# The last block's up-projection by seven Strassen products instead of eight, with the weight sums made in the blocks before

## The chip, the cores and the metric

The kernel runs on one core of a Trainium2 chip. The metric is the device time in microseconds of one execution, the median of several runs. Its engines are named as in the profile: PE is TensorE's matmul, PEld its weight load, DVE is VectorE, ACT is ScalarE, POOL is GpSimd, and SP is SyncE, from whose queue every DMA is issued.

## What is computed

The reference is one encoder layer over 2048 positions of 1024 channels: a norm, a windowed attention and a state-space mixer side by side, an output projection, and then a feed-forward part. The change is in the up-projection of the last part:

```python
h = rmsnorm(x, norm2_g[l])
u = dwconv(h @ w_up[l].astype(h.dtype), ffn_conv_w[l], ffn_conv_b[l])
gate, val = jnp.split(u, 2, axis=-1)
x = x + (jax.nn.silu(gate) * val) @ w_down[l].astype(h.dtype)
```

`h` has 1024 channels, `w_up` 2 x 2816 columns, and `dwconv` is a convolution over three positions. All is float32.

## The kernel before

Matmuls keep float32 accuracy by a split: each operand is a rounded part `hi` and a rest `lo`, and `mm3` (lines 106 to 108 of the profile) issues three matmuls, hi by hi, hi by lo and lo by hi, for each 128 channels.

The positions are cut into four blocks `j` of 512. For each block the feed-forward part goes through 22 pairs of 128 columns (one gate, one value). `up_mm` multiplies a pair's two weight tiles with the block's `h2` (8 chunks of 128 channels, so 2 x 8 x 3 = 48 matmuls over 512 positions) into two PSUM banks, tiles `up`. `up_unit` then makes the convolution from the banks: ACT writes the middle tap (line 1049), DVE adds the two others (line 1047, "taps", each out = u x weight + out) and the seam to the block before (from `hal`, one or two elements), ACT makes the tanh, DVE two products (lines 1070 and 1071) and, after a cast on ACT, the rest (line 1075). The result `f` goes into the down-projection `down_unit`, which adds to `x`. Pairs come in groups, and the down-projection of a group stands behind the up-projection of the next one. In the last block each down-projection is cut into halves of 258 and 256 positions (`down_part`, line 1111).

Weights come by DMA as 128x1024 tiles `wraw`. `w_split` makes `whi` on ACT (line 141) and `wlo` on POOL (line 142), two tiles ahead, in two buffers each. `wplan` lists the tiles in order, and `next_w` steps through it.

In blocks 0 to 2 the attention and state-space chunks of the following block are stepped in between by `pace`. At the end of a block `wo_unit` makes the output projection of the next one, and `h2_stage` its norm and the split of its `h2` (line 1022 and line 208), between the last down-projections. The last block has nothing after it but `final` of block 2 (line 1183), and it ends with `last_down`.

The order of the instructions on each engine is set when the program is built, by the framework's scheduler, from the order of the code and its own estimates. An engine executes its instructions strictly in that order.

Of the kernel before, what the change touches and what calls it, by code (L numbers as in the profile page):

```python
# [17 lines left out]
P = 128  # L18
# [39 lines left out]
def block_kernel(ctx: ExitStack, tc: tile.TileContext, a: dict, out: bass.AP):  # L58
# [31 lines left out]
    def dram(name, shape):  # L90
        return dpool.tile(shape, F32, tag=name, name=name)
# [922 lines left out]
    def h2_stage(j, ss):  # L1014
# [10 lines left out]
            split(hi[:, k], lo[:, k], t, eng(14) if k % 2 == 0 else eng(15))  # L1025
        h2[j] = (hi, lo)

    def up_mm(j, pr, ws):
# [48 lines left out]
        pend.append(tail)  # L1077

    def down_unit(j, g, cp, fs, w):
        k0, nk = GROUPS[g]  # L1080
        whi, wlo = w
        x1 = xone[j]
        if j < NB - 1:
            ps = new_mm(f"dn{j}_{g}_{cp}")
            for i in range(2):
                for k in range(nk):
                    kk = ksl(i * nk + k)
                    mm3(ps[i], whi[:, kk], wlo[:, kk], fs[:, k, 0, :TB], fs[:, k, 1, :TB], k == 0, k == nk - 1)
# [7 lines left out]
    PART = ((0, 258), (258, FW))  # L1096

    def down_part(j, g, c, b, fs, w):
        k0, nk = GROUPS[g]
# [94 lines left out]
    def w_wo():  # L1194
        return [(a["w_out"][c], 1024) for c in range(NK)]

    def w_dn(g):
        k0, nk = GROUPS[g]
        return [(a["w_dn"][cp][:, :, k0 * P : (k0 + nk) * P], 2 * nk * P) for cp in range(4)]

    def wo_pair(cp, s):
# [12 lines left out]
                wplan.append((a["w_ch"][int(tok[1:])], 1024))  # L1214
    wplan += [wo_pair(cp, 1) for cp in range(4)]
    wplan += [(a["w_ch"][c], 1024) for c in (11, 12)]
    for j in range(NB):
        for g, (k0, nk) in enumerate(GROUPS):
            wplan += [(a["w_up"][k0 + i, q], 1024) for i in range(nk) for q in range(2)]
            if g > 0:  # L1220
                wplan += w_dn(g - 1)
        if j + 1 < NB:
            wplan[-2:-2] = w_wo()
        wplan += w_dn(len(GROUPS) - 1)

    def step(streams, n=1):
        for _ in range(n):
# [138 lines left out]
    for j in range(NB):  # L1366
# [1 line left out]
        if j > 0:  # L1368
            mx = start_side(j + 1)
        fss = []  # L1370
        for g, (k0, nk) in enumerate(GROUPS):
# [127 lines left out]
```

## Time and profile before

| | us |
|---|---|
| median of 3 runs (2495.41 to 2500.74) | 2496.29 |
| the profiled execution, its own time | 2505.61 |
| its span, first to last instruction | 2503.8 |
| PE busy in the span | 2373.5 |
| DVE, ACT, POOL busy | 1761.6, 1088.3, 1126.9 |
| blocks 0 to 2 of the feed-forward part | 659 to 2110 |
| block 3 | 2110 to the end |

Busy time of PE is modelled and overlaps, so the rate of matmuls is read from start to start. Durations of POOL are rough. The spans of the blocks are read from the sequence of PE's tiles.

### The profile page before, as it was taken

What the parts mean: (1) busy time and instruction counts of PE and PEld (TensorE: products, weight loads), DVE (VectorE), ACT (ScalarE), POOL (GpSimd) and SP (SyncE); (2) the same over time, 40 slices, a digit from 0 to 9 for tenths busy, and PEclk for the clock granted to TensorE, in tenths of its full rate; (3) what the DMA queues carried; (4) which work ended last, traced back from release to release, by engine and by line L of the source; (5) the groups of instructions that cost most, each with busy time, mean ns of one, the idle gap of its engine ahead of it and who ended that gap; (6) DMA issues with size and microseconds to landing.
All of it is one profiled execution on the core that took longest, in us unless ns stands there. A gap on an engine that the chain in (4) does not pass through costs nothing.

```text
span 2503.8 us, 31565 instructions
## 1 busy us (share of the span) xinstructions
PE 2373.5 (95%) x11440; PEld 1975.7 (79%) x11440; DVE 1761.6 (70%) x3116; ACT 1088.3 (43%) x1814; POOL 1126.9 (45%) x625
## 2 busy tenths in 40 slices
PE   8998999887899999999999999999999999999997
PEld 6877798766688887777788777777888877788887
DVE  5778778878786775468978685689686555844445
ACT  5444565444354444335444443254444433433334
POOL 1045314564545435445444443554444445544444
PEclk9999999998899999999999999999999999999998
DMA  6567445774433343333434333343443232332232
GB/s 225 178 198 224 126 147 186 247 246 149 141 116 122 127 140 97 101 112 122 126 131 137 99 133 114 90 129 119 129 127 96 84 114 89 118 101 93 93 94 84
DMA packets 176047, 332.13 MB, mean 133 GB/s; under 512 B 13202, under 2 KB 84242, under 8 KB 175892
## 3 DMA queue, kind: packets, MB, share of 16 engines
q1 hardware_dynamic: 175892, 330.12, 41.2%
q8 instruction: 90, 1.47, 0.2%
q14 instruction: 65, 0.53, 0.1%
HBM read 284.06 MB, written 44.71 MB: 131 GB/s over the span
## 4 chain that ended last, share of the span: by engine, by line
PE 50%; DVE 9%; POOL 2%; issue 2%; ACT 1%; DMA 1%; DVEq 0%; POOLq 0%; SPq 0%; ACTq 0%
PE up_b L108 9%; PE up_b L107 9%; PE up_b L106 9%; PE dn_b L106 3%; PE dn_b L107 3%; PE dn_b L108 3%; DVE fa L1047 2%; POOL wlo L142 2%; PE dn L107 2%; PE dn L106 2%; PE dn L108 2%; PE wo_b L108 2%; PE wo_b L106 2%; PE wo_b L107 2%; DVE m_lo L972 1%
## 5 line engine op out<-in xcount | busy, mean ns | idle before, releaser
L142 POOL TENSOR_TENSOR wlo<-wraw,whi 128x1024 fp32r<-128x1024 f32 (+1 forms) x306 | 739.0, 2416 | 901.8 <-ACT whi L141 849.8
L108 PE MATMUL up_b<-h_hi,wlo 128*128 128x512 f32 x1392 | 555.3, 399 | 15.9 <-POOL wlo L142 15.8
L107 PE MATMUL up_b<-h_lo,whi 128*128 128x512 f32 x1392 | 553.0, 398 | 4.7 <-DVE h_lo L208 4.7
L106 PE MATMUL up_b<-h_hi,whi 128*128 128x512 f32 x1392 | 554.3, 399 | 1.4 <-ACT whi L141 0.9
L141 ACT CAST whi<-wraw 128x1024 fp32r<-128x1024 f32 (+1 forms) x330 | 338.9, 1027 | 453.0 <-PE up_b L107 117.8
L1047 DVE SCALAR_TENSOR_TENSOR fa<-up_b,fcw,fa 128x511 f32<-128x511 f32 (+2 forms) x396 | 271.4, 686 | 206.1 <-ACT fa L1049 201.7
L108 PEld LDWEIGHTS up_b<-h_hi,wlo 128*128 128x128 f32 x1392 | 264.6, 190 | 79.8 <-POOL wlo L142 21.8
L107 PEld LDWEIGHTS up_b<-h_lo,whi 128*128 128x128 f32 x1392 | 264.3, 190 | 63.3 <-DVE h_lo L208 5.9
L106 PEld LDWEIGHTS up_b<-h_hi,whi 128*128 128x128 f32 x1392 | 264.1, 190 | 60.1 <-ACT whi L141 2.3
L106 PE MATMUL dn_b<-f,whi 128*128 128x512 f32 x528 | 211.4, 400 | 0.4 <-DVE x L1090 0.2
L107 PE MATMUL dn_b<-f,whi 128*128 128x512 f32 x528 | 208.8, 395 | 0.0
L108 PE MATMUL dn_b<-f,wlo 128*128 128x512 f32 x528 | 204.3, 397 | 0.0
L1069 ACT ACTIVATE fth<-fa 128x512 f32<-128x512 f32 (+1 forms) x88 | 55.6, 632 | 217.3 <-DVE fa L1047 165.3
L1074 ACT CAST f<-fth 128x512 fp32r<-128x512 f32 (+1 forms) x88 | 54.4, 620 | 207.6 <-DVE fth L1071 169.2
L1090 DVE TENSOR_TENSOR x<-x,dn_b 128x512 f32<-128x512 f32 x144 | 97.5, 680 | 61.0 <-PE dn_b L108 60.9
L1049 ACT ACTIVATE fa<-up_b,fcw 128x512 f32<-128x512 f32 x176 | 136.0, 774 | 0.2
L106 PEld LDWEIGHTS dn_b<-f,whi 128*128 128x128 f32 x528 | 99.7, 189 | 22.8 <-DVE x L1090 1.1
L108 PEld LDWEIGHTS dn_b<-f,wlo 128*128 128x128 f32 x528 | 99.3, 188 | 22.4 <-POOL wlo L142 0.3
L107 PEld LDWEIGHTS dn_b<-f,whi 128*128 128x128 f32 x528 | 99.2, 188 | 21.2
L875 DVE SCALAR_TENSOR_TENSOR ab<-ab,ldt,mask 128x128 f32<-128x128 f32 x256 | 106.7, 482 | 11.7 <-DMA ab<-acs_d 11.5
L1075 DVE TENSOR_TENSOR f<-fth,f 128x512 fp32r<-128x512 f32 (+1 forms) x88 | 79.2, 900 | 30.3 <-ACT f L1074 29.4
L106 PE MATMUL pj_b<-h_hi,whi 128*128 128x512 f32 x208 | 85.4, 411 | 12.3 <-ACT h_hi L235 7.1
(328 smaller groups left out, 5047.1 us busy)
## 6 DMA issues: line engine op xcount, KB each, us to landing
wraw<-in_w_up SPq DMA_DIRECT2D x176, 512.0 KB
wraw<-in_w_dn SPq DMA_DIRECT2D x64, 512.0 KB
wraw<-in_w_out SPq DMA_DIRECT2D x36, 512.0 KB
ab<-acs_d SPq DMA_DIRECT2D x32, 512.0 KB
wraw<-in_w_ch SPq DMA_DIRECT2D x28, 512.0 KB
wraw<-in_w_dn SPq DMA_DIRECT2D x32, 384.0 KB
ak<-ks_d SPq DMA_DIRECT2D x14, 768.0 KB
cs<-in_rope SPq DMA_DIRECT2D x20, 512.0 KB
```

The costliest lines, as they stand in the source:

```text
L106: nc.tensor.matmul(ps, whi, xhi, start=first, stop=False)
L107: nc.tensor.matmul(ps, whi, xlo, start=False, stop=False)
L108: nc.tensor.matmul(ps, wlo, xhi, start=False, stop=last)
L141: A.copy(hi[:, :m], raw[:, :m])
L142: (V if i < WV or i in WVS else G).tensor_tensor(lo[:, :m], raw[:, :m], hi[:, :m].bitcast(F32), ALU.subtract)
L875: (G if i < SUBP[0 if first else 1] else V).scalar_tensor_tensor(ab[:, i, d], ab[:, i, d], ldt[:, d, c, h : h + 1], mask3[:, 2 * d * P : ( ...
L1047: V.scalar_tensor_tensor(o, src, w(q), o, ALU.mult, ALU.add)
L1049: A.activation(ai[:, 0:TB], u, AF.Identity, bias=w(3), scale=w(2))
L1069: A.activation(th[:, :n], acc[:, 0, :n], AF.Tanh)
L1074: A.copy(fs[:, idx, 0, :n], th[:, :n])
L1075: V.tensor_tensor(fs[:, idx, 1, :n], th[:, :n], fs[:, idx, 0, :n].bitcast(F32), ALU.subtract)
L1090: V.tensor_tensor(xv, xv, ps[i], ALU.add)
```

## The change

In block 3 two pairs make a "super" `s` (11 of them). Its weights are seen as a 2 x 2 matrix: gate or value by the first or second 512 channels. Its `h2` is a 2 x 2 matrix too: first or second 512 channels by first or second 256 positions. A Strassen scheme in Winograd's form makes the four result quarters from seven products. `up_super` issues them: each has 2 x 4 x 3 = 24 matmuls over 256 positions into one bank, with one 128x1024 weight tile. Three of the seven tiles are weights as they are, four are sums `S1` to `S4`. One copy on ACT and eight additions on DVE (line 1111 of the changed kernel; six take one bank each, one bank is taken twice) build the gate tile `us..g` and the value tile `us..v` in SBUF. `up_unit` is as before, but its input `u` is now such a tile, and the two units of a super are emitted inside the next super.

The weight sums are made on POOL in blocks 0 to 2, behind the split of a pair's value tile, for the pairs with `pr % 3 == j`: four operations of 128x512 for each of 22 pairs, and two DMAs to the scratch `ws_d`. `wraw` has three buffers instead of two. In block 3 weights are split three tiles ahead instead of two, and the third pair of buffers lies in the attention's. `h2_stage_w` makes the seven split combinations of `h2` for block 3 in place of the plain split. The groups of block 3 are of 4, 4, 4, 4, 4 and 2 pairs instead of 4, 4, 4, 4, 3 and 3. The DMA scratch of the program is set smaller.

```diff
+GROUPSW = [(0, 4), (4, 4), (8, 4), (12, 4), (16, 4), (20, 2)]
+PROD = (0, 2, 3, 1, 6, 4, 5)
...
-        raw = wpool.tile([P, 1024], F32, tag="wraw", name="wraw")
+        raw = wpool.tile([P, 1024], F32, tag="wraw", name="wraw", bufs=3)
...
+        elif i >= wdeep[0] and (i - wdeep[0]) % 3 == 2:
+            hi = bp.tile([P, H * P], F32R, tag="qs", name="whi3")
+            lo = bp.tile([P, 12 * P], F32R, tag="ks", name="wlo3")
...
+        if i in wsum:
+            gate, val = wraws[i - 1], raw
+            g0, g1, v0, v1 = gate[:, :512], gate[:, 512:], val[:, :512], val[:, 512:]
+            sa, sb = (sumpool.tile([P, 2, 512], F32, tag="wsum", name=f"ws{wsum[i]}{z}") for z in "ab")
+            G.tensor_tensor(sa[:, 0], v0, v1, ALU.add)
+            G.tensor_tensor(sa[:, 1], sa[:, 0], g0, ALU.subtract)
+            G.tensor_tensor(sb[:, 0], g0, v0, ALU.subtract)
+            G.tensor_tensor(sb[:, 1], g1, sa[:, 1], ALU.subtract)
+            nc.sync.dma_start(ws_d[wsum[i], :, 0:2], sa)
+            nc.sync.dma_start(ws_d[wsum[i], :, 2:4], sb)
...
+        if i >= wdeep[0]:
+            w_split(i + 2)
+            w_raw(i + 3)
...
+    def h2_stage_w(j, ss):
...
+            tt = t1024(f"h2s{j}_{k}").rearrange("p (z n) -> p z n", z=4)
+            V.tensor_tensor(tt[:, 0], b12, b11, ALU.subtract)
+            V.tensor_tensor(tt[:, 1], b22, tt[:, 0], ALU.subtract)
+            G.tensor_tensor(tt[:, 2], b22, b12, ALU.subtract)
+            G.tensor_tensor(tt[:, 3], b21, tt[:, 1], ALU.subtract)
+            split(pw[0][:, 0, 0, k], pw[0][:, 0, 1, k], b11, V)
+            split(pw[1][:, :, 0, k], pw[1][:, :, 1, k], tt[:, 0:2], V)
+            split(p6[0][k // 2][:, k % 2], p6[1][k // 2][:, k % 2], b21, V)
+            split(pw[2][:, :, 0, k], pw[2][:, :, 1, k], tt[:, 2:4], G)
+            split(pw[0][:, 1, 0, k], pw[0][:, 1, 1, k], b22, V)
...
+    def up_super(j, s, prev):
...
+            for pr in range(2):
+                for k in range(4):
+                    hi, lo = h2[j][PROD[q]][k]
+                    mm3(bank[:, pr], w[0][:, ksl(4 * pr + k)], w[1][:, ksl(4 * pr + k)], hi, lo, k == 0, k == 3)
...
+        A.copy(gl, product(0))
+        add(gr, gl, product(1))
+        if prev:
+            prev.pop(0)()
+        add(vl, gr, product(2))
+        ps = product(3)
+        add(vr, vl, ps)
+        add(gr, gr, ps)
+        add(gl, gl, product(4))
+        if prev:
+            prev.pop(0)()
+        add(gr, gr, product(5))
+        add(vl, vl, product(6))
```

What the built program makes of it is shown at three places. The first is DVE in block 3, in the convolution of a pair (`up3_9_b0` and `_b1` are its two banks, `fa` the convolution, `hal` the seam). Before:

```order
L1047 SCALAR_TENSOR_TENSOR fa3_9_18378<-up3_9_b0_18328,fcw_139,fa3_9_18378 128x510
L1047 SCALAR_TENSOR_TENSOR fa3_9_18378<-up3_9_b0_18328,fcw_139,fa3_9_18378 128x511
L1056 TENSOR_SCALAR fa3_9_18378<-up3_9_b0_18328,fcw_139 128x1
L1047 SCALAR_TENSOR_TENSOR fa3_9_18378<-hal_93,fcw_139,fa3_9_18378 128x2
L1047 SCALAR_TENSOR_TENSOR fa3_9_18378<-up3_9_b0_18328,fcw_139,fa3_9_18378 128x1
L1047 SCALAR_TENSOR_TENSOR fa3_9_18378<-hal_93,fcw_139,fa3_9_18378 128x1
L1070 SCALAR_TENSOR_TENSOR fth3_9_18396<-fth3_9_18396,fa3_9_18378 128x514
L1047 SCALAR_TENSOR_TENSOR fa3_9_18378<-up3_9_b1_18329,fcw_139,fa3_9_18378 128x510
L1047 SCALAR_TENSOR_TENSOR fa3_9_18378<-up3_9_b1_18329,fcw_139,fa3_9_18378 128x511
```

After the change, from the last addition of super 4 to the first of super 5 (`us3_4g` and `us3_4v` are its gate and value tiles, `us3_5_1` is the bank of the next super's product 1, `fa3_8` and `fa3_9` its two pairs' convolutions):

```order
L1111 TENSOR_TENSOR us3_4v_18836<-us3_4v_18836,us3_4_6_19080 128x2x256
L1147 SCALAR_TENSOR_TENSOR fa3_9_19291<-us3_4g_18835,fcw_143,fa3_9_19291 128x511
L1147 SCALAR_TENSOR_TENSOR fa3_8_19172<-hal_96,fcw_143,fa3_8_19172 128x2
L1147 SCALAR_TENSOR_TENSOR fa3_9_19291<-hal_96,fcw_143,fa3_9_19291 128x2
L1147 SCALAR_TENSOR_TENSOR fa3_8_19172<-hal_96,fcw_143,fa3_8_19172 128x1
L1147 SCALAR_TENSOR_TENSOR fa3_8_19172<-us3_4v_18836,fcw_143,fa3_8_19172 128x510
L1147 SCALAR_TENSOR_TENSOR fa3_9_19291<-hal_96,fcw_143,fa3_9_19291 128x1
L1147 SCALAR_TENSOR_TENSOR fa3_9_19291<-us3_4v_18836,fcw_143,fa3_9_19291 128x510
L1147 SCALAR_TENSOR_TENSOR fa3_8_19172<-us3_4v_18836,fcw_143,fa3_8_19172 128x511
L1147 SCALAR_TENSOR_TENSOR fa3_9_19291<-us3_4v_18836,fcw_143,fa3_9_19291 128x511
L1147 SCALAR_TENSOR_TENSOR fa3_8_19172<-hal_96,fcw_143,fa3_8_19172 128x2
L1111 TENSOR_TENSOR us3_5g_19106<-us3_5g_19106,us3_5_1_19146 128x2x256
```

The taps of a pair now read a tile in SBUF where they read a bank, and the rest of the taps of two pairs stands ahead of the addition that empties the bank of the next super's product 1.

The second place is POOL in block 0 (`wlo` is the split of a weight tile, `ws9a` and `ws9b` are the sums of pair 9, `y` and `arc` belong to the state-space mixer and the attention). Before:

```order
L142 TENSOR_TENSOR wlo_6675<-wraw_6626,whi_6674 128x1024
L900 TENSOR_TENSOR y6_7000<-xsbf6_6846,vecs_143 128x512
L142 TENSOR_TENSOR wlo_6723<-wraw_6678,whi_6722 128x1024
L142 TENSOR_TENSOR wlo_6762<-wraw_6726,whi_6761 128x1024
L796 TENSOR_TENSOR arc5_6840<-arc5_6840,mhalf_83 128x1
L142 TENSOR_TENSOR wlo_6768<-wraw_6765,whi_6767 128x1024
L142 TENSOR_TENSOR wlo_6879<-wraw_6771,whi_6878 128x1024
```

After the change:

```order
L158 TENSOR_TENSOR wlo_6703<-wraw_6654,whi_6702 128x1024
L929 TENSOR_TENSOR y6_7036<-xsbf6_6874,vecs_147 128x512
L158 TENSOR_TENSOR wlo_6751<-wraw_6706,whi_6750 128x1024
L164 TENSOR_TENSOR ws9a_6910<-wraw_6799 128x512
L166 TENSOR_TENSOR ws9b_6911<-wraw_6793,wraw_6799 128x512
L158 TENSOR_TENSOR wlo_6790<-wraw_6754,whi_6789 128x1024
L825 TENSOR_TENSOR arc5_6868<-arc5_6868,mhalf_86 128x1
L165 TENSOR_TENSOR ws9a_6910<-ws9a_6910,wraw_6793 128x512
L158 TENSOR_TENSOR wlo_6796<-wraw_6793,whi_6795 128x1024
L167 TENSOR_TENSOR ws9b_6911<-wraw_6793,ws9a_6910 128x512
L158 TENSOR_TENSOR wlo_6907<-wraw_6799,whi_6906 128x1024
```

Two sums stand ahead of the split of the tile before the pair's, one behind it and one behind the next.

The third place is DVE at the end of block 2 (`dn2_5` are banks of the last down-projection, `h2t3` is the normed input of block 3, `h2w3` its split, `h2s3` the differences). Before:

```order
L1090 TENSOR_TENSOR x1_2_12816<-x1_2_12816,dn2_5_0_b0_17154 128x512
L1022 SCALAR_TENSOR_TENSOR h2t3_17116<-x1_3_16760,gv_110,r2_3_17107 128x512
L1022 SCALAR_TENSOR_TENSOR h2t3_17120<-x1_3_16760,gv_110,r2_3_17107 128x512
L1022 SCALAR_TENSOR_TENSOR h2t3_17124<-x1_3_16760,gv_110,r2_3_17107 128x512
L1090 TENSOR_TENSOR x1_2_12816<-x1_2_12816,dn2_5_0_b1_17155 128x512
L208 TENSOR_TENSOR h2_3_lo_17115<-h2t3_17116,h2_3_hi_17114 128x512
L1090 TENSOR_TENSOR x1_2_12816<-x1_2_12816,dn2_5_1_b0_17182 128x512
L208 TENSOR_TENSOR h2_3_lo_17115<-h2t3_17124,h2_3_hi_17114 128x512
L1022 SCALAR_TENSOR_TENSOR h2t3_17128<-x1_3_16760,gv_110,r2_3_17107 128x512
```

After the change:

```order
L1190 TENSOR_TENSOR x1_2_12940<-x1_2_12940,dn2_5_0_b0_17383 128x512
L1074 SCALAR_TENSOR_TENSOR h2t3_17301<-x1_3_16940,gv_114,r2_3_17287 128x512
L1074 SCALAR_TENSOR_TENSOR h2t3_17303<-x1_3_16940,gv_114,r2_3_17287 128x512
L1074 SCALAR_TENSOR_TENSOR h2t3_17320<-x1_3_16940,gv_114,r2_3_17287 128x512
L1190 TENSOR_TENSOR x1_2_12940<-x1_2_12940,dn2_5_0_b1_17384 128x512
L1080 TENSOR_TENSOR h2s3_0_17305<-h2t3_17301 128x256
L237 TENSOR_TENSOR h2w3_0_17294<-h2t3_17301,h2w3_0_17294 128x256
L237 TENSOR_TENSOR h2w3_pl0_17299<-h2t3_17303,h2w3_ph0_17297 128x256
L1080 TENSOR_TENSOR h2s3_1_17324<-h2t3_17320 128x256
L237 TENSOR_TENSOR h2w3_0_17294<-h2t3_17303,h2w3_0_17294 128x256
L1190 TENSOR_TENSOR x1_2_12940<-x1_2_12940,dn2_5_1_b0_17411 128x512
L237 TENSOR_TENSOR h2w3_0_17294<-h2t3_17320,h2w3_0_17294 128x256
```

Between the additions to `x` stand more and shorter operations, and all of them but those additions read only tiles in SBUF.

## Rows read from the trace of the kernel before

**Rows 1.** The page: busy time by engine, and what DMA moved in each slice.

```profile
PE 2373.5 (95%) x11440; PEld 1975.7 (79%) x11440; DVE 1761.6 (70%) x3116; ACT 1088.3 (43%) x1814; POOL 1126.9 (45%) x625
...
GB/s 225 178 198 224 126 147 186 247 246 149 141 116 122 127 140 97 101 112 122 126 131 137 99 133 114 90 129 119 129 127 96 84 114 89 118 101 93 93 94 84
```

**Rows 2.** Stretches: length, busy PE, PEld, DVE, ACT, POOL; PEclk, DMA share, GB/s.

```profile
659.00:1130.00 471.00, 462.25 (x2079) 376.00 (x2078) 316.96 (x529) 196.87 (x318) 223.24 (x114) 0.99 0.37 118
...
1620.00:2110.00 490.00, 475.75 (x2146) 387.65 (x2144) 355.46 (x645) 208.98 (x347) 230.86 (x119) 0.98 0.35 111
...
2229.00:2273.30 44.30, 44.30 (x194) 35.93 (x193) 21.88 (x57) 17.58 (x23) 19.29 (x8) 1.00 0.29 90
2273.30:2296.30 23.00, 23.00 (x194) 23.00 (x193) 10.77 (x23) 5.28 (x6) 9.61 (x4) 1.00 0.31 101
```

**Rows 3.** Timeline of PE: the first matmul of each stretch of 192.

```profile
2228.79 0.39 PE L106 MATMUL up_b<-h_hi,whi 128*128 128x512 f32 x1
...
2273.16 0.28 PE L106 MATMUL dn<-f,whi 128*128 128x258 f32 x1
...
2296.27 0.40 PE L106 MATMUL up_b<-h_hi,whi 128*128 128x512 f32 x1
```

**Rows 4.** DVE in block 3, 2206 to 2452, groups by shape.

```profile
L1047 DVE SCALAR_TENSOR_TENSOR fa<-up_b,fcw,fa 128x511 f32<-128x511 f32 x28 | 21.0, 749 | 0.8
...
L1075 DVE TENSOR_TENSOR f<-fth,f 128x514 fp32r<-128x514 f32 x14 | 15.8, 1131 | 6.8 <-ACT f L1074 6.8
L1111 DVE TENSOR_TENSOR x<-x,dn 128x258 f32<-128x258 f32 x32 | 13.5, 423 | 22.6 <-PE dn L108 22.6
...
L1070 DVE SCALAR_TENSOR_TENSOR fth<-fth,fa 128x514 f32<-128x514 f32 x15 | 10.4, 695 | 11.4 <-ACT fth L1069 11.4
...
L1047 DVE SCALAR_TENSOR_TENSOR fa<-up_b,fcw,fa 128x1 f32<-128x1 f32 x28 | 5.9, 212 | 0.0
```

**Rows 5.** Timeline of DVE at the end of block 2.

```profile
2105.05 1.40 DVE L1022 SCALAR_TENSOR_TENSOR h2t<-x,gv,r 128x512 f32<-128x512 f32 x2
2106.37 0.67 DVE L1090 TENSOR_TENSOR x<-x,dn_b 128x512 f32<-128x512 f32 x1
...
2111.83 2.23 DVE L1022 SCALAR_TENSOR_TENSOR h2t<-x,gv,r 128x512 f32<-128x512 f32 x1
```

**Rows 6.** Timeline of POOL in the same stretch.

```profile
2109.11 1.65 POOL L208 TENSOR_TENSOR h_lo<-h2t,h_hi 128x512 fp32r<-128x512 f32 x1 [1.28 <-ACT h_hi L207]
2110.72 2.79 POOL L142 TENSOR_TENSOR wlo<-wraw,whi 128x1024 fp32r<-128x1024 f32 x1
```

**Rows 7.** Timeline of DVE in block 2, around 1875 us.

```profile
1874.44 2.81 DVE L1047 SCALAR_TENSOR_TENSOR fa<-hal,fcw,fa 128x2 f32<-128x2 f32 x2
```

**Rows 8.** Timeline of POOL at the same time.

```profile
1874.85 2.38 POOL L142 TENSOR_TENSOR wlo<-wraw,whi 128x1024 fp32r<-128x1024 f32 x1
```

**Rows 9.** Timeline of DVE in block 3, around 2253 us.

```profile
2252.75 1.53 DVE L1047 SCALAR_TENSOR_TENSOR fa<-up_b,fcw,fa 128x510 f32<-128x510 f32 x2 [1.99 <-ACT fa L1049]
```

**Rows 10.** Timeline of POOL at the same time.

```profile
2252.12 2.41 POOL L142 TENSOR_TENSOR wlo<-wraw,whi 128x1024 fp32r<-128x1024 f32 x1 [3.13 <-ACT whi L141]
```

**Rows 11.** POOL in blocks 0 to 2, 660 to 2110, groups by shape.

```profile
L142 POOL TENSOR_TENSOR wlo<-wraw,whi 128x1024 fp32r<-128x1024 f32 x200 | 493.0, 2466 | 571.5 <-ACT whi L141 547.7 <-PE stf L618 4.0 <-PE pt L763 3.9
L142 POOL TENSOR_TENSOR wlo<-wraw,whi 128x768 fp32r<-128x768 f32 x24 | 46.7, 1948 | 61.6 <-ACT whi L141 57.9 <-DMA wraw<-in_w_out 3.7
...
L924 POOL TENSOR_TENSOR y<-y,zs 128x512 f32<-128x512 f32 x12 | 15.5, 1292 | 0.7
```

**Rows 12.** Timeline of ACT at the end of block 2: the norm's factor arrives.

```profile
2096.86 0.59 ACT L185 COPY r<-r_pr 128x512 f32<-128x512 f32 x1 [3.28 <-PE r_pr L183]
```

**Rows 13.** Timeline of PE: the first matmuls of block 3.

```profile
2110.04 0.50 PE L106 MATMUL up_b<-h_hi,whi 128*128 128x512 f32 x1
...
2113.57 0.50 PE L108 MATMUL up_b<-h_hi,wlo 128*128 128x512 f32 x1 [2.79 <-POOL wlo L142]
```

**Rows 14.** Busy time by stretch, columns as in Rows 2: the clock behind that wait.

```profile
2116.00:2120.00 4.00, 4.00 (x14) 3.16 (x13) 0.00 (x0) 0.18 (x1) 2.45 (x2) 0.72 0.18 50
```

More of the change, by code (lines that the diff above doesn't have):

```diff
@@ L1026, in h2_stage @@
         h2[j] = (hi, lo)
+    def h2_stage_w(j, ss):
+        x1 = xone[j]
+        sc = rstd_cols(ss, TB, D, f"r2_{j}")
+        yield
+        r = rstd_bcast(sc, f"r2_{j}")
+        pw = [
+            big.tile([P, SLOT], F32R, tag="big", name=f"h2w{j}_{q}")[:, : 16 * HT]
+            .rearrange("p (z s k n) -> p z s k n", z=2, s=2, k=4) for q in range(3)
+        ]
+        p6 = [
+            [bp.tile([P, 2, HT], F32R, tag=tag, name=f"h2w{j}_{tag}{q}", bufs=2) for q in range(2)]
+            for tag in ("ph", "pl")
+        ]
+        for k in range(4):
+            hs = []
+            for kk in (k, k + 4):
+                t = t512(f"h2t{j}")[:, :TB]
+                V.scalar_tensor_tensor(
+                    t, x1[:, kk, 1 : TB + 1], gv[:, 1, kk : kk + 1], r[:, :TB], ALU.mult, ALU.mult
+                )
+                hs.append(t)
+            b11, b12, b21, b22 = (h[:, z * HT : (z + 1) * HT] for h in hs for z in range(2))
+            tt = t1024(f"h2s{j}_{k}").rearrange("p (z n) -> p z n", z=4)
[8 more added lines that the diff above has]
+            split(pw[0][:, 1, 0, k], pw[0][:, 1, 1, k], b22, V)
+        b = [[(pw[q][:, z, 0, k], pw[q][:, z, 1, k]) for k in range(4)] for q in range(3) for z in range(2)]
+        b.append([(p6[0][k // 2][:, k % 2], p6[1][k // 2][:, k % 2]) for k in range(4)])
+        h2[j] = [b[0], b[2], b[3], b[4], b[1], b[5], b[6]]
@@ new lines, in up_super, with product, add @@
+    def up_super(j, s, prev):
+        name = f"us{j}_{s}"
+        ug = bp.tile([P, 8, P], F32, tag="ab", name=f"{name}g", bufs=2).rearrange("p a n -> p (a n)")
+        ug = ug.rearrange("p (i n) -> p i n", i=2)
+        uv = sumpool.tile([P, 2, 512], F32, tag="wsum", name=f"{name}v")
+        gl, gr, vl, vr = ug[:, :, :HT], ug[:, :, HT:], uv[:, :, :HT], uv[:, :, HT:]
+        def product(q):
+            w = next_w()
+            bank = psm.tile([P, 512], F32, tag="mm", name=f"{name}_{q}")
+            bank = bank.rearrange("p (i n) -> p i n", i=2)
+            for pr in range(2):
+                for k in range(4):
+                    hi, lo = h2[j][PROD[q]][k]
+                    mm3(bank[:, pr], w[0][:, ksl(4 * pr + k)], w[1][:, ksl(4 * pr + k)], hi, lo, k == 0, k == 3)
+            return bank
+        def add(o, x, y):
+            V.tensor_tensor(o, x, y, ALU.add)
+        A.copy(gl, product(0))
[11 more added lines that the diff above has]
+        add(vl, vl, product(6))
+        return ug, uv
@@ L1079, in down_unit @@
     def down_unit(j, g, cp, fs, w):
-        k0, nk = GROUPS[g]
+        k0, nk = groups(j)[g]
         whi, wlo = w
@@ L1216, in block_kernel, with w_prod @@
     wplan += [(a["w_ch"][c], 1024) for c in (11, 12)]
-    for j in range(NB):
-        for g, (k0, nk) in enumerate(GROUPS):
-            wplan += [(a["w_up"][k0 + i, q], 1024) for i in range(nk) for q in range(2)]
+    def w_prod(s):
+        two = slice(2 * s, 2 * s + 2)
+        up = lambda q, z: a["w_up"][two, q, :, 512 * z : 512 * z + 512]
+        raw = {"11": up(0, 0), "12": up(0, 1), "22": up(1, 1)}
+        for q in range(4):
+            raw[f"S{q + 1}"] = ws_d[two, :, q]
+        for nm in ("11", "S2", "S3", "S1", "12", "S4", "22"):
+            wplan.append((raw[nm].rearrange("c p n -> p c n"), 1024))
+    for j in range(NB):
+        for g, (k0, nk) in enumerate(groups(j)):
+            if j in BW:
+                for s in range(k0 // 2, (k0 + nk) // 2):
+                    w_prod(s)
+            else:
+                for pr in range(k0, k0 + nk):
+                    wplan += [(a["w_up"][pr, q], 1024) for q in range(2)]
+                    if pr % 3 == j:
+                        wsum[len(wplan) - 1] = pr
             if g > 0:
-                wplan += w_dn(g - 1)
+                wplan += w_dn(g - 1, j)
         if j + 1 < NB:
             wplan[-2:-2] = w_wo()
-        wplan += w_dn(len(GROUPS) - 1)
+        wplan += w_dn(len(GROUPS) - 1, j)
     def step(streams, n=1):
@@ L1370, in block_kernel @@
         fss = []
-        for g, (k0, nk) in enumerate(GROUPS):
+        if j in BW:
+            wdeep[0] = wpos[0]
+        prev = []
+        for g, (k0, nk) in enumerate(groups(j)):
             fs = big.tile([P, SLOT], F32R, tag="big", name=f"f{j}_{g}").rearrange(
@@ L1386, in block_kernel @@
                 i = 2
+            if j in BW:
+                for s in range(k0 // 2, (k0 + nk) // 2):
+                    ug, uv = up_super(j, s, prev)
+                    for i in range(2):
+                        prev.append(
+                            lambda pr=2 * s + i, fs=fs, idx=2 * s + i - k0, u=[ug[:, i], uv[:, i]]:
+                            up_unit(j, pr, fs, idx, u)
+                        )
+                    step([fin], 5)
+                i = nk
             for i in range(i, nk):
@@ L1393, in block_kernel @@
             if g == len(GROUPS) - 1:
+                for f in prev:
+                    f()
                 flush()
```

22 lines of the change are left out of this document (15 added, 7 removed).

## The prediction

> **What bounds the kernel now.** I read the page first for the whole: PE is busy for 95% of the span [rows 1]. Next come the busy times by stretch: in block 3 PE is busy for all of 44.30 us and all of 23.00 us, and in blocks 0 to 2 for about 97% (475.75 of 490.00) [rows 2]. So in block 3 the time is the number of matmuls times their distance, unless another engine falls behind. The timeline of PE gives the distance from start to start: 192 matmuls over 512 positions took 2273.16 - 2228.79 = 44.37 us, 0.2311 us each, and 192 over 258 and 256 positions took 2296.27 - 2273.16 = 23.11 us, 0.1204 us each [rows 3]. The short ones cost 4% more than half.
>
> Next I looked for an engine that could fall behind. POOL is busy for 19.29 of 44.30 us in block 3 [rows 2] and idles 3.13 us ahead of a `wlo`, waiting for ACT [rows 10]; ACT itself waits until PE frees the buffers. That is much spare time, and DVE has as much. But the timelines show that the two don't run freely beside each other. A DVE operation of two elements, mean 0.21 us for its like [rows 4], stands twice in 1874.44 to 1877.25 [rows 7], and `wlo` on POOL ended at 1874.85 + 2.38 = 1877.23 [rows 8]: both waited for it. An `h2t` of 0.70 us (two in 1.40) took 2.23 us while POOL ran its `wlo`, and that `wlo` took 2.79 us in place of 2.41; `h_lo` ahead of it took 1.65 in place of 1.29 [rows 5, 6, 10, 11]. The slowed DVE operations read two large or small operands from SBUF. One whose input is a PSUM bank isn't slowed: two taps took 1.53 us within a `wlo`, and an addition from `dn_b` took its 0.67 [rows 5, 9, 10]. In block 3 the last product of a unit, which reads SBUF alone, has a mean of 1131 ns, the first, of the same size, 695 [rows 4].
>
> The Trainium skill, SBUF — State Buffer, in its section on the two sides of SBUF, says why: a DVE operation with two SBUF inputs and a GpSimd operation share one pair of ports, the first to start holds it for the whole instruction, and the other blocks. The trace agrees (2.23 us for 0.70), and the rule speaks against a change that moves taps from PSUM to SBUF.
>
> **The change, part by part.**
>
> **Matmuls of block 3.** Removed: 22 pairs of 48 matmuls over 512 positions, 1056 x 0.2311 = 244.0 us. Added: 11 supers of 7 x 24 over 256, 1848 x 0.1204 = 222.4 us. Saved: **22 us**. The distance of short matmuls is that of the down halves, at a granted clock of 1.00 [rows 2, 3].
>
> The Trainium skill, TensorE: Matmul & The Clock Gate, in the part on back-to-back matmuls, gives N/2.4 ns and some 2.5 ns for each; by it 512 columns take 215.8 ns and 256 take 109.2, and the saving would be 227.9 - 201.8 = 26 us. The rows are 7 to 10% slower than the page at both widths, so I go by them.
>
> **Work beside the matmuls in block 3.** Two supers and one down-projection between take 2 x 168 x 0.1204 + 192 x 0.1204 = 63.6 us on PE. In that time POOL splits 14 + 4 tiles, 18 x 2.41 = 43.4 us [rows 10]. DVE has four pairs: per pair four taps, now from SBUF, and three products (28 operations of 0.70 to 0.75 us), and six seam operations of 0.21 (24) [rows 4]. Less what can lie in POOL's waits at the start of a `wlo`, I count 0.55 us of exclusive time for each large and 0.1 for each small one, 18 us. Together 61 of 63.6 us: that just fits if all interleaves without loss, so the lower bound is 0.
>
> It can't interleave freely, since each engine executes in order. In the order of the changed kernel, five to eight taps and six seam operations stand ahead of the addition that empties the bank of the next super's product 1. PE has four banks, so it can run five products, 5 x 24 x 0.1204 = 14.4 us, before it needs that one. In those 14.4 us POOL runs a `wlo` for each product (2.89 us each), and 2.89 - 2.41 leaves about one DVE operation between two: five of the eight taps. Three taps, the seams and one `wlo` are left, and then the addition, some 7 us late. Six supers directly follow another: 42 us. In each of the five down-projections the cover is four banks of 12 matmuls, 5.8 us, and the DVE and POOL work that stands ahead is about 12, so 6 us late: 30 us. That walk gives 72. The upper bound lets DVE never overlap POOL, since one blocked operation also holds those behind it: DVE's own 28 x 0.70 + 24 x 0.21 + 8 x 0.27 + 14 x 0.68 (additions of 512) + 16 x 0.42 (down) = 43, with 18 x 2.3 = 84 us against 63.6, and with 5.2 such periods, 110 us. I take **+60**, below the walk, because PE's lateness also gives POOL longer pauses in which DVE catches up.
>
> **The end of block 2.** `h2_stage_w` starts when the norm's factor is there, 2096.86 + 0.59 = 2097.45 [rows 12]. Product 0 needs no difference, but the later ones need all. DVE's own work to the last `b11` part is 7 x 0.70 + 8 x 0.67 + 16 x 0.42 + 2 x 0.68 = 18.4, so 2115.9 if POOL never interferes. Before, the block started at 2110.04 and stood 2.79 us for a `wlo` at once, so at 2112.8 in effect [rows 13]: lower bound +3. At the other end the differences and splits on POOL queue with its `wlo`: 3 x 1.95 + 4 x 2.47 + 8 x 0.65 (half of 1.29) + 5 x 1.29 = 27 us [rows 11], and DVE's two-SBUF operations in turn with them, 7 x 0.70 + 16 x 0.42 = 12: 2097.45 + 39 = 2136.5, +24 [rows 11]. Three products (8.7 us) can be run meanwhile, which makes it +15. PE's clock adds to that: behind the 2.79 us of before it stood at 0.72, between its two levels of 1.2 and 2.4 GHz [rows 14]. I take **+14**, the middle.
>
> **Weight sums.** Four operations of 128x512 for 22 pairs, 88 x 1.29 = 113.5 us on POOL in blocks 0 to 2 [rows 11]. It is busy there for 223.24 to 230.86 us of a block [rows 2], and idles 571.5 / 200 = 2.86 us ahead of a `wlo`, waiting for the cast, and that for PE [rows 11]. The order puts two sums, 2.58 us, ahead of one `wlo`, and one each ahead of the next two: within the 2.86, so the lower bound is 0. If the wait for the value tile's DMA or a DVE operation pushes them together, four sums pass one pause, (5.16 - 2.86) x 22 = 50 us. They also hold DVE operations with two SBUF operands. I take **+12**, nearer the idle time, for something like half a microsecond a pair.
>
> **Costed at nothing.** The groups of block 3 hold the same 22 pairs; the last down-projection shrinks, the one before grows. ACT casts 33 more tiles, but is busy for 17.58 of 44.30 us. Raw tiles come at 7 x 0.524 MB in 20.2 us, 182 GB/s; a slice of the page reached 247 [rows 1], the third buffer covers a late one, and without that cover each late tile would stop PE. The 44 writes of `ws_d` are on no path to PE until block 3. On SP they stand in front of the next raw loads, and wait there for POOL's sums; that cost is in the +12.
>
> **Sum:** -22 + 60 + 14 + 12 = **+64**. The profiled execution's own time is 9.3 us above the median of the runs (2505.61 against 2496.29), with the same work, so I add the differences to the median: 2496.3 + 64 = **2560 us**.
>
> **The rivals.**
>
> Contention hidden (faster). If DVE works off its taps in the pauses, and the down-projections (one `wlo` per 5.8 us) let it catch up, steady stalls stay near 0, the boundary costs 3 and the sums 5: 2496 - 22 + 8 = 2482. For it: 61 fits in 63.6. Against it: taps stand in front of the additions. It decides where stalls and the other terms together stay under 22 us, 2 us a super.
>
> Contention partial. Steady 20, boundary 8, sums 2: 2496 - 22 + 30 = 2504. For it: PE gives four banks of slack. Against it: the walk.
>
> DVE never beside POOL. 110 + 24 + 25 - 22: 2633. For it: DVE is in order, and the 2.81 us for two tiny operations [rows 7]. Against it: additions from PSUM run beside a `wlo` [rows 5].
>
> That the change doesn't do what it says is out: the order holds the 1848 matmuls.
>
> **How the numbers follow.** Main case 0.60 (own range 2525 to 2600), hidden 0.12, partial 0.16, never 0.12. A change under 0.2%, 5 us, can't be told from none. Partial spreads from 2488 to 2520: 0.01 of it faster, 0.04 the same, 0.11 slower. So faster 0.13, same 0.04, slower 0.83. The range, 2488 to 2625, leaves out most of the hidden case, half of the last, and the tails.
>
> **What would show it.** In the profile after: distance of matmuls over 256 positions near 0.120; taps in block 3 above 1.2 us in place of 0.749; PE's waits in block 3 released by DVE's additions (line 1111), not by DMA; `wlo` there above 2.6 us; block 3 longer than before, not 22 us shorter; the first product near its old start but PE waiting on `h2w` parts behind it; few waits on `wlo` in blocks 0 to 2, 12 us in sum. The prediction is wrong if taps keep near 0.75 us, if waits point at ACT or DMA, or if the PE stalls in block 3 sum to less than 22 us.

## The result, and the profile after

The changed kernel takes 2591.56 us (median of 4), the kernel before 2495.85 beside it: 1.038 times as long, 95% interval 1.0359 to 1.040. That is 95.7 us more. The forecast was 2560 with a range of 2488 to 2625.

First the page of the changed kernel, busy time by engine; it answers to [rows 1].

```profile
PE 2382.5 (92%) x12232; PEld 2020.6 (78%) x12232; DVE 1949.1 (75%) x3213; ACT 1128.8 (44%) x1870; POOL 1347.3 (52%) x754
```

POOL shows 220 us more, about its 88 sums and 33 tiles more to split. DVE shows 187 us more, where its 77 new additions at 0.68 us need 52 (seven a super; the section on the change says eight additions, six of them with a bank of their own, but it is seven and five). Where PE waits in block 3 is in the view of waits, from 2126 us to the end: us in total, times, longest.

```profile
PE us L118 <- ACT whi L157: 26.9, 9, 5.4
PE dn L118 <- DVE x L1211: 14.7, 9, 2.7
PE us L120 <- POOL wlo L158: 11.4, 7, 2.9
PE us L118 <- DVE us_2g L1111: 8.5, 1, 8.5
PE n_pr L1251 <- POOL n_c L1248: 4.5, 2, 3.6
PE us L119 <- DVE h2w L237: 4.1, 3, 2.1
```

Before, PE stood 9.9 us in block 3, most of it in the final norm. Block 3 began at 2126.47 and not at 2110.04 [rows 13], and took 465.5 us in place of 393.8. The profiled execution before was itself 9 us above its median, so the two profiles are only 88.2 us apart; in the profile of the run with the writes alone (below), which took 2498 us and has block 3 unchanged, block 3 began at 2103.46. The places of the loss are read from the first matmul of each stretch on PE. The first super took 39.7 us in place of 20.2, the next three 31.0, 35.5 and 28.9. Behind that a cycle repeats: a super of 20, one of 28.4, a down-projection of 26.5 to 28.0 in place of 23.1. Summed over block 3, PE is 102 us over its matmuls at 0.1204 us each.

The busy times of one cycle and of the first super (columns as in [rows 2]):

```profile
2289.50:2365.70 76.20, 68.38 (x530) 67.58 (x529) 58.38 (x94) 29.94 (x36) 45.38 (x18) 0.93 0.39 125
2126.50:2166.20 39.70, 27.46 (x170) 25.48 (x169) 27.55 (x33) 16.69 (x27) 33.09 (x20) 0.74 0.28 93
```

In the cycle DVE shows 58 us for its 94 operations, and in the first super the clock was granted at 0.74, between the levels of 1.2 and 2.4 GHz, behind the waits there. The cause is seen in the timelines of one slow super. DVE, ACT and POOL of the changed kernel, from 2315 to 2332 us (start, time, operation; in brackets the engine's idle time ahead of it and what ended that):

```profile
2316.93 0.21 DVE L1147 SCALAR_TENSOR_TENSOR fa<-hal,fcw,fa 128x1 f32<-128x1 f32 x1
2317.06 4.17 DVE L1147 SCALAR_TENSOR_TENSOR fa<-us_4v,fcw,fa 128x510 f32<-128x510 f32 x3
2321.15 2.33 DVE L1147 SCALAR_TENSOR_TENSOR fa<-hal,fcw,fa 128x2 f32<-128x2 f32 x1
2323.40 0.67 DVE L1111 TENSOR_TENSOR us_5g<-us_5g,us 128x512 f32<-128x512 f32 x1
2324.00 2.36 DVE L1170 SCALAR_TENSOR_TENSOR fth<-fth,fa 128x514 f32<-128x514 f32 x1
...
2326.55 0.68 DVE L1170 SCALAR_TENSOR_TENSOR fth<-fth,fa 128x514 f32<-128x514 f32 x1
...
2328.48 0.68 DVE L1171 TENSOR_TENSOR fth<-fth,fa 128x514 f32<-128x514 f32 x1
```

```profile
2319.23 1.98 ACT L157 CAST whi<-wraw 128x1024 fp32r<-128x1024 f32 x2
2328.00 0.62 ACT L1174 CAST f<-fth 128x514 fp32r<-128x514 f32 x1 [6.79 <-DVE fth L1171]
2329.20 0.62 ACT L1174 CAST f<-fth 128x514 fp32r<-128x514 f32 x1 [0.58 <-DVE fth L1171]
2329.72 1.99 ACT L157 CAST whi<-wraw 128x1024 fp32r<-128x1024 f32 x2
```

```profile
2317.87 7.95 POOL L158 TENSOR_TENSOR wlo<-wraw,whi 128x1024 fp32r<-128x1024 f32 x3 [4.39 <-ACT whi L157]
2330.84 5.31 POOL L158 TENSOR_TENSOR wlo<-wraw,whi 128x1024 fp32r<-128x1024 f32 x2 [5.02 <-ACT whi L157]
```

```profile
2330.82 0.39 PE L118 MATMUL us<-h2w,whi 128*128 128x256 f32 x1 [2.61 <-ACT whi L157]
```

While POOL makes its three `wlo` from 2317.87 to 2325.8, DVE gets hardly more than one operation with two SBUF operands through for each, and the one of two elements takes 2.33 us. In all of block 3 there are 88 taps: the 50 that meet no operation of POOL have a mean of 739 ns, the other 38 of 1671. The product `fth` is late by that. On ACT the casts of `f`, which need `fth`, stand ahead of the next two `whi`: ACT idles 6.79 us ahead of the first of them. POOL then idles 5.02 us for `whi`, and PE 2.61 us (the last row). So an engine that is 30 of 76 us busy passes DVE's lateness on to PE.

### The profile page after: what moved, and what is told of

It reads as the page before. It is cut to its first block, busy times and chain, and to the rows that moved or that the text cites. A ratio compares the mean times of both kernels' runs of the same rounds, so it can differ in the third digit from the quotient of the medians.

```text
span 2592.0 us, 33692 instructions
## 1 busy us (share of the span) xinstructions
PE 2382.5 (92%) x12232; PEld 2020.6 (78%) x12232; DVE 1949.1 (75%) x3213; ACT 1128.8 (44%) x1870; POOL 1347.3 (52%) x754
## 4 chain that ended last, share of the span: by engine, by line
PE 46%; DVE 20%; issue 4%; POOL 3%; ACT 2%; DMA 1%; SPq 0%; DVEq 0%; ACTq 0%; POOLq 0%
DVE fa L1147 7%; PE up_b L120 6%; PE up_b L118 6%; PE up_b L119 6%; PE dn_b L118 4%; PE dn_b L119 4%; PE dn_b L120 4%; POOL wlo L158 2%; PE wo_b L120 2%; PE wo_b L118 2%; PE wo_b L119 2%; PE us L118 2%; PE us L119 2%; PE us L120 1%; DVE ab L904 1%
## 5 line engine op out<-in xcount | busy, mean ns | idle before, releaser
L158 POOL TENSOR_TENSOR wlo<-wraw,whi 128x1024 fp32r<-128x1024 f32 (+1 forms) x339 | 832.3, 2459 | 765.4 <-ACT whi L157 744.8
L120 PE MATMUL up_b<-h_hi,wlo 128*128 128x512 f32 x1040 | 418.4, 402 | 15.6 <-POOL wlo L158 15.6
L118 PE MATMUL up_b<-h_hi,whi 128*128 128x512 f32 x1040 | 416.2, 401 | 7.1 <-ACT whi L157 5.2
L119 PE MATMUL up_b<-h_lo,whi 128*128 128x512 f32 x1040 | 415.4, 400 | 2.0 <-DVE h_lo L237 2.0
L1147 DVE SCALAR_TENSOR_TENSOR fa<-up_b,fcw,fa 128x510 f32<-128x510 f32 (+1 forms) x264 | 196.4, 745 | 104.2 <-ACT fa L1149 101.3
L118 PE MATMUL us<-h2w,whi 128*128 128x256 f32 x528 | 159.3, 302 | 25.7 <-ACT whi L157 17.0
L120 PE MATMUL us<-h2w,wlo 128*128 128x256 f32 x528 | 157.2, 301 | 11.5 <-POOL wlo L158 11.4
L119 PE MATMUL us<-h2w,whi 128*128 128x256 f32 x528 | 157.7, 299 | 4.1 <-DVE h2w L237 4.1
L118 PEld LDWEIGHTS us<-h2w,whi 128*128 128x128 f32 x528 | 109.7, 208 | 28.2 <-ACT whi L157 18.5
L1147 DVE SCALAR_TENSOR_TENSOR fa<-hal,fcw,fa 128x1 f32<-128x1 f32 (+1 forms) x264 | 119.5, 460 | 4.6
L120 PEld LDWEIGHTS us<-h2w,wlo 128*128 128x128 f32 x528 | 108.8, 207 | 13.3 <-POOL wlo L158 13.2
```

The lines of the kernel that those rows point to most:

```text
L119: nc.tensor.matmul(ps, whi, xlo, start=False, stop=False)
L120: nc.tensor.matmul(ps, wlo, xhi, start=False, stop=last)
L1147: V.scalar_tensor_tensor(o, src, w(q), o, ALU.mult, ALU.add)
```

## The experiments

All ratios are to the kernel before, run on the same chip. The changed kernel stands at 1.038.

**The port: no `wlo`.**

```diff
+        if i >= wdeep[0]:
+            wdone[i] = (hi, hi)
+            return
         (V if i < WV or i in WVS else G).tensor_tensor(lo[:, :m], raw[:, :m], hi[:, :m].bitcast(F32), ALU.subtract)
```

> The changed kernel without the split's rest in block 3: `wlo` is not made there and `whi` is used in its place, so POOL has almost nothing to do in block 3 while PE has the same matmuls. In the changed kernel the 11 supers and six down-projections take 102 us more than their matmuls at 0.1204 us: 19 in the first super, 35 in the next three, 41 in the cycles behind, 6 at the end. Theory (DVE operations with two SBUF operands can't run beside a POOL operation, and all lateness comes from that): taps in block 3 fall from about 1.3 us to 0.75, PE's waits on ACT's `whi` and on DVE fall to under 10 us in block 3 (without the first super), and the time falls by 65 to 85 us, to 2507 to 2527. Rival (DVE has too much work of its own in block 3, or stands in a bad order, POOL or not): taps get faster, but PE's waits stay, and the time falls by under 30, to above 2560.

This kernel leaves out the rest of the weights in block 3, so its result is less exact; PE has the same matmuls. Measured: 2507.89 us, 1.0045 (1.0033 to 1.0056), so 84 us came back. A cycle of the trace without `wlo`, busy times as above:

```profile
2246.90:2309.70 62.80, 62.80 (x531) 62.80 (x530) 38.60 (x94) 30.41 (x36) 0.00 (x0) 1.00 0.48 151
```

The same 94 operations of DVE take 38.60 us in place of 58.38, and PE doesn't stop. Over block 3 the 88 taps have a mean of 747 ns in place of 1141. PE's waits in block 3 are now:

```profile
PE n_pr L1254 <- POOL n_c L1251: 4.2, 2, 3.3
PE us L120 <- POOL wlo L161: 2.9, 1, 2.9
PE us L119 <- DVE h2w L240: 2.4, 2, 2.2
PE us L118 <- ACT whi L157: 2.3, 1, 2.3
```

All of the product waits are in the first super, which still takes 36.5 us. With `wlo` gone, DVE's own work and order don't make PE wait behind the first super; the rival falls. What this run alone can't say is whether the port or merely the missing step in the weight path did it.

**More slack on the weight path.**

```diff
-        elif i >= wdeep[0] and (i - wdeep[0]) % 3 == 2:
+        elif i >= wdeep[0] and (i - wdeep[0]) % 4 == 3:
+            hi = bp.tile([P, 1024], F32R, tag="xsb", name="whi4", bufs=2)
+            lo = bp.tile([P, 1024], F32R, tag="xsb", name="wlo4", bufs=2)
+        elif i >= wdeep[0] and (i - wdeep[0]) % 4 == 2:
...
             w_raw(i + 3)
+            w_split(i + 3)
+            w_raw(i + 4)
```

> The changed kernel with a fourth pair of weight buffers in block 3, split four tiles ahead; the POOL work is the same. In the trace after, PE waits in every second super 2.4 us for a `wlo` and 2.6 us for a `whi` whose cast stands on ACT behind an operation that waits for DVE. Theory of the order on ACT (the weight path has only 2.3 us of slack and stands behind DVE on ACT's queue): another product of slack, 2.9 us, covers these waits of 2.4 to 2.6 us, so block 3 loses some 40 us less: 2545 to 2560. Theory of the port alone (DVE and POOL together have 61 of 63.6 us to do, so whatever is covered here comes back as a wait on a bank): under 15 us, 2577 to 2595.

Measured: 2587.71 us, 1.0362 (1.033 to 1.0395), against 1.038 within the intervals. PE's waits in block 3, the first rows:

```profile
PE dn L118 <- DVE fa L1152: 20.1, 5, 5.0
PE us L118 <- ACT whi L160: 20.1, 6, 6.6
PE dn L120 <- POOL wlo L161: 5.4, 3, 1.8
```

A part of the waits took another place: behind `whi` the products waited 20.1 us and no longer 26.9, and 20.1 us now stand ahead of the down-projection's matmuls, released by DVE's taps, where 1.2 stood. ACT's order moves the lateness, and the time stays. The theory of the order on ACT falls.

**Half, and all, of `wlo` on DVE.** The selection reads, for all: `V if i < WV or i in WVS or i >= wdeep[0] else G`; for half there is `and (i - wdeep[0]) % 2` with it.

> The changed kernel with every second `wlo` of block 3 on DVE instead of POOL. Alone, a `wlo` takes 1.22 us on DVE in the trace before and 2.41 on POOL. Theory of the port: for two supers and a down-projection the time in which one of the two engines shuts the other out falls from 61 to 51 us of 63.6 (9 x 2.41 + 9 x 1.22 + 18), and about half of the 84 us that the first experiment gave back comes back: 2540 to 2565. Rival (DVE's own work is what is late, and it gets 11 us more of it for each 63.6): 2592 to 2620.

> The changed kernel with every `wlo` of block 3 on DVE. Theory of the port: nothing on POOL shuts DVE out; DVE itself has 43 + 18 x 1.22 = 65 us of work for 63.6 of matmuls, so it is the bound by a little and its order costs some: 2520 to 2560. Rival (DVE's own work decides): above 2592.

Measured: half, 2564.89 us, 1.0266 (1.0236 to 1.0296); all, 2523.41 us, 1.0105 (1.0089 to 1.0122). DVE was given 119 us of work more and the kernel became 68 us shorter. The group of `wlo` on DVE, in block 3 of the second run:

```profile
L158 DVE TENSOR_TENSOR wlo<-wraw,whi 128x1024 fp32r<-128x1024 f32 x96 | 119.1, 1244 | 10.7 <-ACT whi L157 10.7
```

Taps fell to 742 ns, as without `wlo`, though the step still stands in the weight path. It is half as long there, but more slack for that path gave nothing in the run above. So it is POOL's turn at the port, and not the step. With half of them on DVE the taps stood at 873 ns. The some 15 us by which the second run stays above the one without `wlo` aren't taken apart here.

**`wlo` in two operations.**

```diff
+        for z in (slice(0, m // 2), slice(m // 2, m)) if i >= wdeep[0] else (slice(0, m),):
+            (V if i < WV or i in WVS else G).tensor_tensor(lo[:, z], raw[:, z], hi[:, z].bitcast(F32), ALU.subtract)
```

> The changed kernel with each `wlo` of block 3 made by two operations of half the size, which leave DVE a turn between them. POOL's time grows a little (2 x 1.29 for 2.41). Theory (the sum of what the two engines do in turn is what is late): 2585 to 2605. Rival (only the length of one wait is late, since a tap stands for up to 2.4 us and the addition behind it too): 2550 to 2580.

Measured: 2589.61 us, 1.0362 (1.0338 to 1.0386), within the intervals of the changed kernel. A half took:

```profile
L159 POOL TENSOR_TENSOR wlo<-wraw,whi 128x512 fp32r<-128x512 f32 x192 | 272.4, 1444 | 126.0 <-ACT whi L157 120.4 <-PE dn L120 5.3 <-DMA wraw<-in_w_up 0.3
```

Two halves are 2.89 us, and taps have a mean of 1195 ns. A single wait can be shorter now, but POOL's operations are twice as many and their sum is larger. The time goes with the sum and not with the length of one.

**The weight sums: alone, their writes alone, and everything but them.** Into the kernel before went the sums of the diff above; in the second run the raw tiles were written in place of the sums (against the first run, the other sums cut):

```diff
-            G.tensor_tensor(sa[:, 0], v0, v1, ALU.add)
...
+            sa = gate.rearrange("p (i n) -> p i n", i=2)
+            sb = val.rearrange("p (i n) -> p i n", i=2)
```

In the third run, the changed kernel's `w_prod` reads `up(q % 2, q // 2)` for `ws_d[two, :, q]`, and no sum is made.

> The kernel before with the weight sums made and written in blocks 0 to 2, the third raw buffer and the smaller DMA scratch, and block 3 as it was (the sums are read by nobody). In the changed kernel the end of block 2's output projection came 16.4 us later (2100.6 against 2084.2). Theory (the sums hold up `wlo` and DVE there): 2509 to 2517, 13 to 21 us above before, nearly all in blocks 1 and 2. Rival (that lateness comes from other moved instructions, as those of the third buffer): within 5 us of before, 2492 to 2501.

> The kernel before with the third raw buffer and with 44 writes of 512 KB in blocks 0 to 2, but with no sums: the raw gate and value tiles are written. Sums and writes together cost 26 us. Theory (the operations on POOL cost, by holding up `wlo` and DVE): the time stays within 6 us of before, 2491 to 2504. Rival (the writes or the raw tiles held longer cost): 2512 to 2525.

> The changed kernel without the weight sums and their writes; block 3 loads plain weight quarters in their place, so its work is the same. The sums alone cost the kernel before 26 us. If that cost adds to the one in block 3: 2560 to 2572. If the pauses that the sums force on PE in blocks 0 to 2 are partly the same as those of the changed end of block 2: 2575 to 2585.

Measured: sums alone 2523.39 us, 1.0106 (1.0083 to 1.0129), 26 us above before and twice what I had forecast. Writes alone 2497.27 us, 0.9992 (0.998 to 1.0003): nothing. The changed kernel without sums 2561.65 us, 1.0257 (1.0239 to 1.0275), 30 us less than with them. It is POOL's operations that cost. PE's waits in blocks 0 to 2 of the kernel with the sums alone:

```profile
PE up_b L110 <- POOL wlo L144: 19.1, 15, 2.5
PE wo_b L108 <- DVE x L1102: 10.4, 2, 5.2
PE po L785 <- DVE pl L779: 9.5, 4, 4.9
PE pt L775 <- DVE pl L779: 5.3, 4, 2.1
PE up_b L108 <- ACT whi L143: 3.9, 3, 3.5
PE aps L805 <- DVE ass L802: 3.0, 1, 3.0
```

Before, the same view had 12.0 us for `wlo`, 1.2 for `po` behind `pl`, and 0.9 for `whi`; no `aps` stood there. So 7 us more stand directly behind `wlo`, 3 behind `whi`, and some 12 in the attention, where DVE's `pl` and `ass` are late; 5.5 came back at `yo`. With the writes alone 15.6 us stood behind `wlo`, so about half of those 7 is the sums' own. The part in the attention I hadn't priced: an operation on POOL makes DVE wait, even if it stands in POOL's idle time. The busy times from 659 us to block 3 show it, with the writes alone and then with the sums alone (columns as in [rows 2]):

```profile
659.00:2103.46 1444.46, 1405.27 (x6354) 1141.69 (x6352) 1038.63 (x1827) 612.35 (x1010) 684.74 (x352) 0.99 0.41 132
659.00:2129.36 1470.36, 1413.47 (x6334) 1147.86 (x6334) 1074.04 (x1824) 611.88 (x1009) 800.05 (x436) 0.98 0.40 130
```

DVE has the same work in both, and shows 35 us more.

**The sums on DVE.** In the kernel with every `wlo` of block 3 on DVE, the four operations read `V.` for `G.`.

> The kernel with every `wlo` of block 3 on DVE, and the weight sums on DVE too. A 128x512 operation with two SBUF operands takes 0.68 us on DVE and 1.29 on POOL, so the 88 sums take 60 us instead of 113.5. Theory (what counts is the time in which one of the two engines shuts the other out): the sums' cost falls from 26 to some 13 us, 2505 to 2515. Rival (DVE is the fuller of the two in blocks 1 and 2, about 348 of 445 us against 249, and PE waits there for DVE's `pl`): 2523 to 2545.

Measured: 2533.96 us, 1.0141 (1.0124 to 1.0158), 9 us more than with the sums on POOL. The rival was right. The 88 sums had a mean of 1160 ns on DVE, not 680: 60 took some 0.68 us, and the other 28 all met an operation of POOL. On POOL the mean was 1397 in the changed kernel. That PE's loss comes from DVE being the fuller engine there is the rival's reading; this run shows the time, and waits of PE behind `wlo` (16.0 us) and `pl` as with the sums on POOL.

**The differences of `h2`.**

```diff
-            h2s = (h2_stage_w if j + 1 in BW else h2_stage)(j + 1, ss)
+            h2s = h2_stage(j + 1, ss)
...
+                    z, c = divmod(PROD[q] % 4, 2)
+                    hi, lo = (t[:, 4 * z + k, HT * c : HT * c + HT] for t in h2[j])
```

> The changed kernel with the plain split of `h2` for block 3: the products read quarters of it, and the four differences are left out. The first super took 39.7 us in place of 20.2. Theory (the differences and their splits on DVE and POOL make the first super late): it falls to about 24 us and the time by 13 to 18, to 2574 to 2579. Rival (the first super is late because the last additions of block 2 and the first convolutions stand there too, so the time only moves to the second super): 2584 to 2592.

Measured: 2583.41 us, 1.0346 (1.0323 to 1.037), 8 us less. The first super fell from 39.7 to 27.4 us as expected, but the second rose from 31.0 to 34.6. Both theories were half right.

**The final norm of block 2.** One word: `step([fin], 1)` for `step([fin], 5)`.

> The changed kernel with one step of `final` of block 2 in each super instead of five. In the trace after, eight of its operations stand on DVE in one row (7.46 us) ahead of the addition of product 1 of the third super, and PE waits 8.46 us for it. Theory (that row is late by itself): 5 to 9 us faster, 2583 to 2587, and the third super falls from 35.5 to about 29 us. Rival (DVE has the same sum of work in the first four supers, so the wait only moves): within 3 us, 2589 to 2595.

Measured: 2592.61 us, 1.0378 (1.0363 to 1.0393): no change. The third super fell from 35.5 to 31.1 us, and behind it, where the rest of the norm now stands, the fifth took 21.6 in place of 19.9 and the sixth grew too. The 8.46 us wait was the most visible of the trace and was worth nothing: DVE had the same sum of work.

**The best of it together.** The kernel with every `wlo` on DVE, and

```diff
-                    if pr % 3 == j:
+                    if j == (pr % 3 == 2):
...
-            G.tensor_tensor(tt[:, 2], b22, b12, ALU.subtract)
-            G.tensor_tensor(tt[:, 3], b21, tt[:, 1], ALU.subtract)
+            V.tensor_tensor(tt[:, 2], b22, b12, ALU.subtract)
+            V.tensor_tensor(tt[:, 3], b21, tt[:, 1], ALU.subtract)
```

with the last split of `h2` and the last four `wlo` of block 2 on DVE as well.

> The kernel with every `wlo` of block 3 on DVE (2523 in its own run), and two edits more: the sums are made for 15 pairs in block 0 and 7 in block 1, none in block 2 (with the sums alone, the end of block 0's stage came no later than before, the ends of blocks 1 and 2 came 6.9 and 12.4 us later), and the differences and splits of `h2_stage_w` that were on POOL, with the last four `wlo` of block 2, are on DVE. Theory (time in turn of the two engines, by stage): block 2 gets its 12 us back, block 0 pays some 3 to 5 for the seven pairs more, and the first super (37.7 us there) falls by some 8: 2503 to 2515, still no faster than before. Rival for the sums (block 0 is full with 15): block 0 ends over 10 us later and nothing is gained. Rival for the first super (DVE itself is late there, POOL or not): the first super stays above 36 us. Both rivals: 2520 to 2530.

Measured: 2524.15 us, 1.0099 (1.0082 to 1.0116), as without the two edits. The rival for the sums was right: block 0's output projection began at 1063.5 us, 15 us later than in the run with every `wlo` on DVE, and PE waited there 15.5 us for `pl`, not 6.3:

```profile
PE po L802 <- DVE pl L796: 15.5, 3, 9.0
```

The first super fell from 37.7 to 32.4 us, less than the 8 of the theory but in its direction, and block 3 began 5.8 us later. No version of the change that I ran beats the kernel before.

## Why the prediction was right, and where its sizes were off

**Matmuls, -22 us: right.** In the run without `wlo` a cycle of 528 matmuls took 62.8 us, 0.119 us each, a little under the 0.1204 of [rows 3].

**Contention in block 3, +60: right in cause, too small.** It measured 84 us (first experiment); the walk gave 72. I took less than the walk on the ground that PE's lateness gives POOL pauses in which DVE catches up. That step failed. DVE does catch up in such a pause (2326 to 2331 in the timeline above), but the pause is a stop of PE itself. Of the 13.4 us by which a cycle is longer (76.2 against 62.8), 7.8 are PE's stops; in the rest it is busy for 68.4 us with the same matmuls, at a granted clock of 0.93 over the cycle. I had counted no clock in that term. By the stretches above, the six supers that directly follow another lost 59 us, 35 of them in the first three, where the final norm of block 2 stands too; the walk had 42. The down-projections lost some 22 where it had 30. The Trainium skill, SBUF — State Buffer, in its section on the two sides of SBUF, has the first of the two engines hold the shared ports for its whole instruction; the runs agree, with a mean of 1141 ns for a tap in the kernel with `wlo` and 747 without. Taps stayed just under the 1.2 us that I had named as a sign, and `wlo`, at 2.55, under its 2.6: it is DVE that waits for POOL, far more than POOL for DVE.

**The path was another.** I had PE waiting for the additions that empty banks (line 1111) and wrote that waits pointing at ACT would make me wrong. Only 8.5 us of PE's waits were for such an addition, 26.9 for `whi`. They do point at ACT, but ACT was waiting for DVE, as the timelines show for one super, and when a fourth buffer took some of these waits away, as much lateness appeared at the down-projection. The walk's second path, the down-projection behind its own additions, is there with 14.7 us (line 1211). So for the supers the chain named was wrong and its root was right.

**Weight sums, +12: the term was off by half.** They cost 26 us alone and 30 in the changed kernel. I had compared 2.58 us of sums with 2.86 us of POOL's idle time [rows 11], which treats POOL as an engine of its own, although the same argument in block 3 said that POOL's time is also DVE's. The lower bound of 0 rested on that comparison alone.

**Two readings of the rows.** Of the two tiny operations of [rows 7] only the second waited for that `wlo`: in the trace they run from 1874.44 to 1874.90 and from 1874.94 to 1877.25. And the last product's 1131 ns against 695 for the first [rows 4] isn't explained by what it reads, since both read SBUF alone. In the run without `wlo` each of the three products has a mean of 690 ns within 1, so which of them is slow depends on which one meets a `wlo`.

**End of block 2, +14: nearer 8.** Leaving out the differences gave 8 us; the first super alone lost 12 more than it would have, and 4 of it came back in the next.

The sum by the runs is -22 + 84 + 26 + 8 = 96 us, and 95.7 were measured. The 84 are the changed kernel less the run without `wlo`, so the sum tests only the other three terms: 12 us, where that run stood 11 above the kernel before. That it fits so well is partly luck, as the runs overlap: the sums are 26 or 30 by the run, and the 84 hold 3 us of the first super.

**The rival "DVE never beside POOL"**, 2633, was the nearer description of the cycle, and its steady term of 110 too large. One reason can be seen: additions from PSUM did run beside `wlo` (a mean of 679 ns, against 686 without). **"Contention hidden"** asked for stalls under 22 us. With `wlo` gone from block 3 the kernel still took 11 us more than before, so the sums, at 26, would have decided it by themselves.

## What to carry to other kernels

Count DVE operations with two SBUF operands and POOL's operations as one engine, and add up their time by stage before moving work to POOL's "idle" time or an operand from PSUM to SBUF. A longest wait is a poor guide to a gain: three cures of visible waits (a fourth buffer, a spread norm, shorter `wlo`) moved the wait and gave some 4 us at most, while the one that took time away from the shared port gave 68. And price a scheme that saves multiplications with the additions that it needs: here the 88 sums on POOL alone took back the 22 us of matmuls.

## What I had not expected of the hardware

`wlo` of 128x1024 takes 1244 ns on DVE and 2546 on POOL in block 3, so the fuller engine is the cheaper place: 119 us more on DVE made the kernel 68 us shorter. A 128x512 sum on DVE has a mean of 1160 ns beside POOL's `wlo`, against 680 alone; there the move from POOL to DVE gave nothing back, and the kernel took 9 us more.
